# Token columns that are read alternately from two sets of 128 in a decoder trunk's matmuls

## The chip, the core and the metric

The kernel runs on one core of a Trainium2 chip. The time is the device time of one execution in microseconds (us). The kernel before took 2052.29 us in the median of three runs (2049.8 to 2054.64). TensorE (PE in the profile) multiplies, ScalarE (ACT) and VectorE (DVE) work element by element, GpSimd (POOL) does a few sums and issues some DMAs, SyncE (SP) issues the loads. PEld is the loading of the stationary operand on TensorE.

## The reference

One sequence of 256 tokens with 2048 features, in float32, passes through two layers. Cut to what matters:

```python
for i in range(2):
    h = rmsnorm(x, mix_norm[i])
    x = x + (rglru_block(h) if i == 0 else dilated_attention_block(h))
    h = rmsnorm(x, mlp_norm[i])
    x = x + square(relu(h @ w1[i])) @ w2[i]        # 2048 -> 8192 -> 2048
return rmsnorm(x, final_norm)

# rglru_block:  xb, gb = split(h @ w_in)           # 2048 -> 2 x 2560
#               xb = causal_conv4(xb)
#               r, i = sigmoid(blockdiag(xb, w_a)), sigmoid(blockdiag(xb, w_x))   # 10 blocks of 256
#               scan over the tokens of a * h + u, times gelu(gb), @ w_out
# attention:    q, k, v = h @ w_qkv; partial rotary on q, k; three dilated windows mixed; @ w_o
```

All weights are read once; the output is float32.

## The kernel before, in words

Every product is taken in three matmuls. Both operands are split into a high and a low part of a shorter float type (`fp32r`); high x high, high x low and low x high are added up in a PSUM bank. A weight block of 128 rows by 2048 (1 MB, a *unit*) is loaded into `raw`, ScalarE writes its high part `whi` (L132), VectorE subtracts to give the low part `wlo` (L136). Units run in a written order, with loads five units ahead and the split two to three units ahead.

There are two families of products:

- *Weights stand, tokens move* (`stand_w`, L286). The output is features by tokens. For each of 16 blocks of 128 input features, a 128x128 block of the weights is loaded as the stationary operand and the 256 tokens pass by: `whi` with the tokens' high part, `whi` with their low part, `wlo` with their high part. One unit is 48 matmuls of 256 columns. The projections of the recurrent block (40 units), the first MLP products (64 per layer) and q and k (32) go this way. `gate_run` (L437) does the same with the gates' blocks, 24 matmuls for each of ten heads.
- *Tokens stand, weights move* (`stand_x`, L298). The output is tokens by features; 512 columns of weights pass by. The second MLP products, v and the output projections go this way. Here the weights lie in an order made on the host, so that `in_turn` (L318) reads them alternately from two halves that are 256 elements apart, column by column, and the result comes out in natural order. In the last unit of the program (`last_half`, L957) such matmuls have 256 columns each.

The tokens of a stage lie in four tiles `xT`, each with four blocks of 512 columns: the high parts of 256 tokens, then the low parts. They come from `transpose_chunk` (L234): TensorE transposes 128x128 pieces of the residual `xc` into a PSUM bank `tr`, ScalarE empties it with the norm's scale into `xg` (L244), and `hilo` (L216) writes the high part on ScalarE and the low part on VectorE. For the first stage the transposed input comes from the host. For the gates, `conv_split` (L414) splits the convolution's output `c` into `chl` the same way. In the attention, q and k leave PSUM by two copies of 32 rows on ScalarE (L752, L753) and a product with the rotary table on VectorE (L762).

In the steady part of an MLP, one *group* is eight `stand_w` units and fourteen products of the other family with combined weights (sums of blocks, made on VectorE at L653 and by DMA); VectorE adds the results from the banks into `xc` (L657). Each MLP has seven such groups, after eight `stand_w` units at its start. All three engines run their instructions in the order in which the program writes them.

Of the kernel before, what the change touches and what calls it, by code (L numbers as in the profile page):

```python
# [10 lines left out]
F32 = mybir.dt.float32  # L11
F32R = mybir.dt.float32r
AF = mybir.ActivationFunctionType
# [4 lines left out]
S = 256  # L18
# [7 lines left out]
KD = D // 128  # L26
# [50 lines left out]
def trunk(ctx: ExitStack, tc: tile.TileContext, a: dict, out: bass.AP):  # L77
    nc = tc.nc
# [45 lines left out]
    def new_hi(i):  # L124
        split[i] = (cut_tile(i, "hi", HI_BUFS),)
# [65 lines left out]
    def after(n, fn, *args):  # L191
        later.setdefault(now[0] + n, []).append((fn, args))
# [7 lines left out]
    def mm(o, l, r, start, stop):  # L200
        nc.tensor.matmul(o, l, r, start=start, stop=stop, skip_group_check=True)  # L201
# [6 lines left out]
    def pcol(name, j):  # L208
        at = PC[name][0] + j
        return par[:, at:at + 1]  # L210
# [5 lines left out]
    def hilo(hi_out, lo_out, src):  # L216
        nc.scalar.activation(hi_out, src, AF.Copy)
        nc.vector.tensor_sub(lo_out, src, hi_out.bitcast(F32))  # L218

    def new_xT(n):  # L220
        t = perm.tile([P, 4, 512], F32R, name=f"xT{n}")
        state["xT", n] = t
        return t

    def xT(k):
        return state["xT", k // 4][:, k % 4, :]

    def new_xg(n):
        if scope[0] in ("mlp", "end"):
            t = lru.tile([P, UW], F32, name=("q12", "q22")[n % 2])  # L230
            return t[:, 0:4 * S].rearrange("p (k s) -> p k s", k=4)
        return lru.tile([P, 4, S], F32, name="xg", bufs=2)

    def transpose_chunk(n, gname):  # L234
        state["kick"] = True
        xg = new_xg(n)
        for b in range(2):
            tr = psum.tile([P, 2, S], F32, name="tr", bufs=2)
            for k in range(2):
                c = (2 * b + k) * 128  # L240
                for t in range(NT):
                    nc.tensor.transpose(tr[:, k, t * 128:(t + 1) * 128], xc[n][:, t, c:c + 128], ident)  # L242
            for k in range(2):
                nc.scalar.activation(xg[:, 2 * b + k, :], tr[:, k, :], AF.Identity,  # L244
                                     scale=pcol(gname, 4 * n + 2 * b + k))
        t = new_xT(n)
        for h in range(2):
            s = slice(2 * h, 2 * h + 2)
            hilo(t[:, s, 0:256], t[:, s, 256:512], xg[:, s, :])

    def square_sum(n, ts=range(NT)):
        sq = state["ssq"]
# [33 lines left out]
    def stand_w(ps, u, ks, w_at, first, last):  # L286
        hi, lo = split[u]
        cut = 128 if state.pop("kick", False) else 256
        for j, k in enumerate(ks):
            x = xT(k)  # L290
            s = slice((w_at + j) * 128, (w_at + j + 1) * 128)
            for at in range(0, 256, cut):
                mm(ps[:, at:at + cut], hi[:, s], x[:, at:at + cut], first and j + at == 0, False)
            cut = 256
            mm(ps, hi[:, s], x[:, 256:512], False, False)
            mm(ps, lo[:, s], x[:, 0:256], False, last and j == len(ks) - 1)

    def stand_x(acc, u, get, ks, first, last, ts=range(NT)):  # L298
        hi, lo = split[u]
        state["kick"] = False  # L300
        for j, k in enumerate(ks):
            x = get(k)
            s = slice(j * 512, (j + 1) * 512)
            for t in ts:
                xh, xl = x[:, t * 128:(t + 1) * 128], x[:, 256 + t * 128:256 + (t + 1) * 128]
                end = j == len(ks) - 1
                three(acc[t], xh, xl, hi[:, s], lo[:, s], first and j == 0, last and end,
                      state["border"] and end and t == ts[-1])

    def three(bank, xh, xl, hi, lo, opens, closes, border):  # L310

        mm(bank, xh, in_turn(hi), opens, False)
        mm(bank, xh, in_turn(lo), False, False)
        cut = 256 if border else 512
        for at in range(0, 512, cut):
            mm(bank[:, at:at + cut], xl, in_turn(hi, at, cut), False, closes and at + cut == 512)
# [74 lines left out]
    blk = {}  # L391
# [22 lines left out]
    def conv_split(h):  # L414
        if h == 0:
            lru.tile([P, 112], F32, name="space0")
        t = lru.tile([P, 2, 512], F32R, name="chl")
        if h == 0:
            lru.tile([P, 16], F32, name="space1")
        blk[h, "chl"] = t  # L420
        hilo(t[:, :, 0:256], t[:, :, 256:512], blk[h, "c"])

    def gb_done(h, j, ps):
        if j == 0:
# [12 lines left out]
    def gate_run(h, u):  # L437
        hi, lo = split[u]
        x = blk[h, "chl"]
        gp = [psum.tile([P, 2, S], F32, name="g", bufs=2) for _ in range(2)]  # L440
        for g in range(2):
            for n in range(2):
                for k in range(2):
                    at = (g * 2 + k) * 256 + n * 128
                    s = slice(at, at + 128)
                    mm(gp[g][:, n, :], hi[:, s], x[:, k, 0:256], k == 0, False)
                    mm(gp[g][:, n, :], hi[:, s], x[:, k, 256:512], False, False)
                    mm(gp[g][:, n, :], lo[:, s], x[:, k, 0:256], False, k == 1)
        after(0, gate_sig, h, gp)

    def gate_sig(h, gp):
# [276 lines left out]
    scale = HD ** -0.5  # L728
# [19 lines left out]
    def qk_done(h, w, ps):  # L748


        z = lru.tile([P, S], F32, name="z", bufs=2)
        nc.scalar.activation(z[0:32], ps[32:64, :S], AF.Copy)  # L752
        nc.scalar.activation(z[32:64], ps[0:32, :S], AF.Copy)  # L753
        after(1, qk_turn, h, w, ps, z)

    def qk_turn(h, w, ps, z):
        if w == 0:
            att["qk", h] = lru.tile([P, 2, 512], F32R, name="qk", bufs=2)
        y = lru.tile([P, S], F32, name="y", bufs=2)
        rope = att["rope"]  # L760
        nc.vector.tensor_mul(z[0:64], z[0:64], rope[0:64, 1, :])
        nc.vector.tensor_mul(y, ps[:, :S], rope[:, 0, :])  # L762
        nc.vector.tensor_add(y[0:64], y[0:64], z[0:64])
        t = att["qk", h]
        hilo_later(t[:, w, 0:256], t[:, w, 256:512], y)
        if w:
            after(1, att_s, h)

    def hilo_later(hi, lo, src):
        nc.scalar.activation(hi, src, AF.Copy)  # L770
        at_end(nc.vector.tensor_sub, lo, src, hi.bitcast(F32))
# [214 lines left out]
    first = [None] * FIRST  # L986
# [28 lines left out]
    for n in range(NCH):  # L1015
        x = new_xg(n)
        t = new_xT(n)
        if n:
            w = wts.tile([P, UW], F32, name="raw", bufs=RAW_BUFS)
        parts = [slice(m * 512, (m + 1) * 512) for m in range(FIRST)]  # L1020
        raw[n] = [(s, w[:, s]) for s in parts]
        cols = [slice(0, 2), slice(2, 4)] if n == 0 else [slice(0, 4)]
        loads = parts if n == 0 else [slice(0, 1024), slice(1024, 2048)]
        for i in range(max(len(cols), len(loads))):
            if i < len(cols):
                c = cols[i]
                nc.sync.dma_start(x[:, c, :], a["xT"][:, 4 * n + c.start:4 * n + c.stop, :])
            if n or i:
                nc.sync.dma_start(w[:, loads[i]], units[n]["ap"][:, loads[i]])
            else:  # L1030
                nc.sync.dma_start(par, a["par"])
        new_hi(n)
        new_lo(n)
        order = ("x0", "w0", "x1", "x2", "x3", "w1", "w2", "w3") if n == 0 else (
            "x0", "x1", "x2", "w0", "x3", "w1", "w2", "w3")
        for what in order:
            k = int(what[1])
            if what[0] == "w":
                hi_piece(n, k)
                lo_piece(n, k)  # L1040
                continue
            g = pcol("mix0", 4 * n + k)
            nc.scalar.activation(t[:, k, 0:256], x[:, k, :], AF.Identity, scale=g)
            nc.vector.scalar_tensor_tensor(t[:, k, 256:512], x[:, k, :], g, t[:, k, 0:256].bitcast(F32),
                                           op0=OP.mult, op1=OP.subtract)
        for m in range(FIRST):
            stand_w(first[m][3][:, :S], n, range(4 * n, 4 * n + 4), 4 * m, n == 0, n == NCH - 1)
        if n == 1:
            softplus_parts()
# [31 lines left out]
    for at in range(len(items) - 1, -1, -1):  # L1081
        u = items[at][0]
# [44 lines left out]
def _layout(x, mix_norm, mlp_norm, final_norm, mlp_w1, mlp_w2, lru_w_in, lru_conv_w, lru_conv_b,  # L1127
            lru_w_a, lru_b_a, lru_w_x, lru_b_x, lru_lambda, lru_w_out, attn_w_qkv, attn_w_o):
    c = np.ascontiguousarray
# [13 lines left out]
    def turned(w):  # L1143
# [4 lines left out]
    con, rope = _tables()  # L1148
    x2 = x[0]
# [1 line left out]
    begin = w_in[[0, 1, KR, KR + 1]].reshape(4, 128, NCH, 512).transpose(2, 1, 0, 3)  # L1151
    d = {
        "x": c(x2.reshape(NT, 128, D).transpose(1, 0, 2)),
        "xT": c(x2.T.reshape(KD, 128, S).transpose(1, 0, 2)),
        "par": c(np.concatenate([cols(mix_norm[0]), cols(mix_norm[1]), cols(mlp_norm[0]), cols(mlp_norm[1]),
                                 cols(lru_lambda[0]), cols(lru_b_a[0]), cols(lru_b_x[0]), cols(lru_conv_b[0]),
                                 cols(lru_conv_w[0])], 1)),
# [31 lines left out]
```

## Time and profile before

| | |
|---|---|
| median of the runs | 2052.29 us |
| profiled execution, device time | 2051.29 us |
| its span, first to last instruction | 2049.2 us |
| TensorE busy | 2031.2 us, 14231 matmuls |
| weight loads on TensorE busy | 1910.6 us |
| VectorE busy | 1712.1 us, 1927 instructions |
| ScalarE busy | 1278.3 us, 1388 instructions |
| HBM read | 409.58 MB, 201 GB/s over the span |
| granted TensorE clock | 0.999 of full |

A name such as `acc<-xT,whi` tells the tile that is written, then what is read: the moving operand and the stationary one. "128x256" is the size of what passes by. A matmul's own duration runs from its start to the end of its last result and overlaps the next matmul; how fast matmuls follow one another is read from their starts, or from a piece of the chain that counts them.

### The profile page before, as it was taken

The numbers are of one execution on the slowest core, as the hardware profiler recorded it, in microseconds if no ns is written. First come the engines' busy times: TensorE is split into PE (matmuls) and PEld (weight loads), VectorE is DVE, ScalarE is ACT, GpSimd is POOL, SyncE is SP. The second block draws the span as 40 slices with busy tenths as digits, with TensorE's granted clock in tenths as the row PEclk, the third lists the DMA queues.
The fourth block names the chain that finished last, engine by engine and source line by source line (L and its number), as shares of the span: only waits on it lengthen the run. The fifth ranks groups of instructions, "written<-read, shape, count | busy, mean of one in ns | idle before, by whom it ended". The sixth has DMA issues, their size and how long they took to land.

```text
span 2049.2 us, 33880 instructions
## 1 busy us (share of the span) xinstructions
PE 2031.2 (99%) x14231; PEld 1910.6 (93%) x14231; DVE 1712.1 (84%) x1927; ACT 1278.3 (62%) x1388; POOL 87.1 (4%) x83
## 2 busy tenths in 40 slices
PE   9999999999999999999999999999999999999998
PEld 8999988999999999999899999989999999999997
DVE  7988865799999989998557868756999999999985
ACT  7777775566566666656646556555666666666554
POOL 0111100000000000000000000000000000000001
PEclk9999999999999999999999999999999999999999
DMA  8555565678888788777555555556888887887873
GB/s 305 206 199 195 191 213 197 236 240 247 286 260 261 251 269 267 230 253 246 206 190 171 179 185 178 179 197 229 247 247 278 257 266 243 271 274 231 248 251 147
DMA packets 68920, 472.59 MB, mean 231 GB/s; under 512 B 7584, under 2 KB 7712, under 8 KB 13472
## 3 DMA queue, kind: packets, MB, share of 16 engines
q1 hardware_dynamic: 60560, 411.45, 54.9%
q0 software_dynamic: 8064, 58.72, 14.3%
q8 instruction: 111, 1.82, 0.3%
q14 instruction: 41, 0.34, 0.0%
q10 hardware_dynamic: 144, 0.26, 0.0%
HBM read 409.58 MB, written 2.10 MB: 201 GB/s over the span
## 4 chain that ended last, share of the span: by engine, by line
PE 88%; DVE 5%; issue 3%; ACT 2%; DMA 1%; SPq 0%; ACTq 0%; DVEq 0%
PE acc L201 44%; PE g L201 31%; PE tr L201 13%; DVE wlo L136 2%; ACT whi L132 2%; DVE xc L657 1%; DVE qT L653 1%; DMA q<-in_w 0%; DVE aT L572 0%; PE tr L242 0%; DMA xg<-in_xT 0%; PE tr L820 0%; DVE uu L563 0%; ACT xg L244 0%; DVE xT L218 0%
## 5 line engine op out<-in xcount | busy, mean ns | idle before, releaser
L132 ACT ACTIVATE whi<-raw 128x2048 fp32r<-128x2048 f32 (+1 forms) x309 | 569.0, 1844 | 375.7 <-PE acc L201 201.8
L136 DVE TENSOR_TENSOR wlo<-raw,whi 128x2048 fp32r<-128x2048 f32 (+1 forms) x309 | 677.0, 2196 | 96.4 <-ACT whi L132 95.4
L201 PE MATMUL g<-xT,whi 128*128 128x256 f32 x3649 | 627.7, 277 | 0.0
L201 PEld LDWEIGHTS g<-xT,whi 128*128 128x128 f32 x3649 | 550.5, 188 | 0.0
L201 PE MATMUL g<-xT,wlo 128*128 128x256 f32 x1824 | 504.5, 277 | 0.0
L201 PE MATMUL acc<-xT,whi 128*128 128x256 f32 x2724 | 466.6, 277 | 0.2 <-ACT whi L132 0.2
L201 PEld LDWEIGHTS acc<-xT,whi 128*128 128x128 f32 x2724 | 410.9, 188 | 1.3 <-ACT whi L132 1.1
L201 PE MATMUL acc<-xT,wlo 128*128 128x256 f32 x1360 | 376.3, 277 | 0.4 <-DVE wlo L136 0.4
L201 PEld LDWEIGHTS g<-xT,wlo 128*128 128x128 f32 x1824 | 342.5, 188 | 0.4 <-DVE wlo L136 0.4
L201 PE MATMUL acc<-whi,aT 128*128 128x512 f32 (+1 forms) x1064 | 322.6, 378 | 0.0
L132 ACT ACTIVATE whi<-q 128x2048 fp32r<-128x2048 f32 x112 | 214.7, 1917 | 117.8 <-PE g L201 91.9
L136 DVE TENSOR_TENSOR wlo<-q,whi 128x2048 fp32r<-128x2048 f32 x112 | 256.1, 2287 | 26.9 <-ACT whi L132 26.4
L201 PEld LDWEIGHTS acc<-xT,wlo 128*128 128x128 f32 x1360 | 255.3, 188 | 0.9 <-DVE wlo L136 0.8
L201 PEld LDWEIGHTS acc<-whi,aT 128*128 128x128 f32 x1064 | 200.6, 189 | 27.4
L201 PE MATMUL tr<-whi,sT 128*128 128x512 f32 (+1 forms) x728 | 213.7, 366 | 5.5 <-DVE xc L657 4.6
L201 PE MATMUL acc<-wlo,aT 128*128 128x512 f32 (+1 forms) x532 | 200.8, 377 | 0.0
L132 ACT ACTIVATE whi<-qT 128x2048 fp32r<-128x2048 f32 x56 | 107.5, 1920 | 126.5 <-PE g L201 91.5
L201 PEld LDWEIGHTS tr<-whi,sT 128*128 128x128 f32 x728 | 137.4, 189 | 33.9 <-issue 16.0
L201 PE MATMUL tr<-whi,aT 128*128 128x512 f32 (+1 forms) x462 | 140.1, 373 | 0.0
L136 DVE TENSOR_TENSOR wlo<-qT,whi 128x2048 fp32r<-128x2048 f32 x56 | 128.1, 2287 | 7.2 <-ACT whi L132 5.6
L201 PE MATMUL tr<-wlo,sT 128*128 128x512 f32 x336 | 127.4, 379 | 0.0
L201 PEld LDWEIGHTS acc<-wlo,aT 128*128 128x128 f32 x532 | 100.6, 189 | 13.4
(169 smaller groups left out, 2119.6 us busy)
## 6 DMA issues: line engine op xcount, KB each, us to landing
raw<-in_w SPq DMA_DIRECT2D x172, 1024.0 KB, 7.0
q<-in_w SPq DMA_DIRECT2D x84, 1024.0 KB, 8.1
raw<-in_w_in SPq DMA_DIRECT2D x35, 1024.0 KB, 4.9
raw<-in_w_qk SPq DMA_DIRECT2D x32, 1024.0 KB, 4.8
q<-q POOLq DMA_DIRECT2D x28, 1024.0 KB, 12.5
q<-qT POOLq DMA_DIRECT2D x28, 1024.0 KB, 7.0
raw<-in_w_out SPq DMA_DIRECT2D x20, 1024.0 KB, 4.8
raw<-in_w_v SPq DMA_DIRECT2D x16, 1024.0 KB, 4.8
```

Source lines behind the costliest of these rows:

```text
L132: nc.scalar.activation(split[i][0][:, s], r, AF.Copy)
L136: nc.vector.tensor_sub(split[i][1][:, s], r, split[i][0][:, s].bitcast(F32))
L201: nc.tensor.matmul(o, l, r, start=start, stop=stop, skip_group_check=True)
L653: nc.vector.tensor_add(q[to], q[a], q[b])
L657: (nc.vector.tensor_add if sign > 0 else nc.vector.tensor_sub)(x, x, bank[b])
```

## The change

The moving tokens of the first family are read alternately. In a block of 512 columns there now lie, in this order: the high parts of a first set of 128 tokens, their low parts, the high parts of a second set of 128, their low parts. `moving` reads column by column from the first and the second set, 256 elements apart: first set's column 0, second set's column 0, first set's column 1, and so on. The matmuls are otherwise the same, in the same order, with the same sizes.

For a result in the natural order, the first set must hold the even tokens and the second the odd ones. So the host sends the first `xT` sorted; `transpose_chunk` reads every second column of the bank as it empties it (`by_turn`) in both MLPs' stages; `conv_split` reads every second column of `c`. In the attention's stage the two sets stay the first and the last 128 tokens, since v takes them as stationary blocks; q and k then come out of PSUM alternating, and the two copies and the product with the table (L752, L753, L762) put them back in order by reading every second column. Instructions keep their number and their places on all engines.

```diff
@@ transpose_chunk
             for k in range(2):
-                nc.scalar.activation(xg[:, 2 * b + k, :], tr[:, k, :], AF.Identity,
+                order = halves if gname == "mix1" else by_turn
+                nc.scalar.activation(halves(xg[:, 2 * b + k, :]), order(tr[:, k, :]), AF.Identity,
                                      scale=pcol(gname, 4 * n + 2 * b + k))
...
-            hilo(t[:, s, 0:256], t[:, s, 256:512], xg[:, s, :])
+            hilo(part(t[:, s], 0), part(t[:, s], 1), xg[:, s, :].rearrange("p k (t q) -> p k t q", t=2))
+
+    def by_turn(x):
+        return x.rearrange("p (q t) -> p t q", t=2)
+
+    def halves(x):
+        return x.rearrange("p (t q) -> p t q", t=2)
+
+    def part(x, u):
+        return x.rearrange("p k (t u q) -> p u k t q", t=2, u=2)[:, u]
+
+    def moving(x, u):
+        return x.rearrange("p (t u q) -> p u q t", t=2, u=2)[:, u]
@@ stand_w
+            xh, xl = moving(x, 0), moving(x, 1)
             for at in range(0, 256, cut):
-                mm(ps[:, at:at + cut], hi[:, s], x[:, at:at + cut], first and j + at == 0, False)
+                mm(ps[:, at:at + cut], hi[:, s], xh[:, at // 2:(at + cut) // 2], first and j + at == 0, False)
             cut = 256
-            mm(ps, hi[:, s], x[:, 256:512], False, False)
-            mm(ps, lo[:, s], x[:, 0:256], False, last and j == len(ks) - 1)
+            mm(ps, hi[:, s], xl, False, False)
+            mm(ps, lo[:, s], xh, False, last and j == len(ks) - 1)
@@ stand_x
-                xh, xl = x[:, t * 128:(t + 1) * 128], x[:, 256 + t * 128:256 + (t + 1) * 128]
+                if get is xT:
+                    xh, xl = (x[:, (2 * t + i) * 128:(2 * t + i + 1) * 128] for i in range(2))
+                else:
+                    xh, xl = x[:, t * 128:(t + 1) * 128], x[:, 256 + t * 128:256 + (t + 1) * 128]
@@ conv_split
-        hilo(t[:, :, 0:256], t[:, :, 256:512], blk[h, "c"])
+        hilo(part(t, 0), part(t, 1), blk[h, "c"].rearrange("p k (q t) -> p k t q", t=2))
@@ gate_run
-                    mm(gp[g][:, n, :], hi[:, s], x[:, k, 0:256], k == 0, False)
-                    mm(gp[g][:, n, :], hi[:, s], x[:, k, 256:512], False, False)
-                    mm(gp[g][:, n, :], lo[:, s], x[:, k, 0:256], False, k == 1)
+                    xh, xl = moving(x[:, k], 0), moving(x[:, k], 1)
+                    mm(gp[g][:, n, :], hi[:, s], xh, k == 0, False)
+                    mm(gp[g][:, n, :], hi[:, s], xl, False, False)
+                    mm(gp[g][:, n, :], lo[:, s], xh, False, k == 1)
@@ qk_done
-        nc.scalar.activation(z[0:32], ps[32:64, :S], AF.Copy)
-        nc.scalar.activation(z[32:64], ps[0:32, :S], AF.Copy)
+        nc.scalar.activation(halves(z[0:32]), by_turn(ps[32:64, :S]), AF.Copy)
+        nc.scalar.activation(halves(z[32:64]), by_turn(ps[0:32, :S]), AF.Copy)
@@ qk_turn
-        nc.vector.tensor_mul(y, ps[:, :S], rope[:, 0, :])
+        nc.vector.tensor_mul(halves(y), by_turn(ps[:, :S]), halves(rope[:, 0, :]))
```

The first stage's split (L1043, L1044) writes the new order too, and the host sorts the transposed input.

More of the change, by code (lines that the diff above doesn't have):

```diff
@@ L1042, in trunk @@
             g = pcol("mix0", 4 * n + k)
-            nc.scalar.activation(t[:, k, 0:256], x[:, k, :], AF.Identity, scale=g)
-            nc.vector.scalar_tensor_tensor(t[:, k, 256:512], x[:, k, :], g, t[:, k, 0:256].bitcast(F32),
+            high, low = (part(t, u)[:, k] for u in range(2))
+            nc.scalar.activation(high, halves(x[:, k, :]), AF.Identity, scale=g)
+            nc.vector.scalar_tensor_tensor(low, halves(x[:, k, :]), g, high.bitcast(F32),
                                            op0=OP.mult, op1=OP.subtract)
@@ L1153, in _layout @@
         "x": c(x2.reshape(NT, 128, D).transpose(1, 0, 2)),
-        "xT": c(x2.T.reshape(KD, 128, S).transpose(1, 0, 2)),
+        "xT": c(x2.T.reshape(KD, 128, 128, 2).transpose(1, 0, 3, 2)).reshape(128, KD, S),
         "par": c(np.concatenate([cols(mix_norm[0]), cols(mix_norm[1]), cols(mlp_norm[0]), cols(mlp_norm[1]),
```

## The prediction

> **What bounds the kernel now.** I read the shares of busy time first, then the table of stretches, then the chain that ended last.
>
> ```profile
> PE 2031.2 (99%) x14231; PEld 1910.6 (93%) x14231; DVE 1712.1 (84%) x1927; ACT 1278.3 (62%) x1388; POOL 87.1 (4%) x83
> PE 88%; DVE 5%; issue 3%; ACT 2%; DMA 1%; SPq 0%; ACTq 0%; DVEq 0%
> 448.00:529.00 81.00, 80.61 (x560) 75.43 (x558) 75.65 (x73) 50.41 (x42) 3.42 (x4) 1.00 0.82 260
> ```
>
> TensorE is busy 99% of the span and carries 88% of the chain. The third row is one of the 14 like groups of the two MLPs (stretch, its length, then PE, PEld, DVE and ACT busy): PE idles 0.4 us of 81, VectorE 5.35 us. The granted clock is 1.00. So time is the number of matmuls times the interval at which they start, and only that interval can move it. VectorE is next in line.
>
> The changed products are these groups (the by-form list, whose last columns are busy us, mean ns of one, idle before):
>
> ```profile
> L201 PE MATMUL g<-xT,whi 128*128 128x256 f32 x3647 | 627.4, 277 | 0.0
> L201 PE MATMUL g<-xT,wlo 128*128 128x256 f32 x1824 | 504.5, 277 | 0.0
> L201 PE MATMUL acc<-xT,whi 128*128 128x256 f32 x2716 | 465.6, 277 | 0.2 <-ACT whi L132 0.2
> L201 PE MATMUL acc<-xT,wlo 128*128 128x256 f32 x1360 | 376.3, 277 | 0.4 <-DVE wlo L136 0.4
> L201 PE MATMUL g<-chl,ghi 128*128 128x256 f32 x160 | 28.7, 281 | 0.0
> L201 PE MATMUL g<-chl,glo 128*128 128x256 f32 x80 | 22.5, 281 | 0.0
> ```
>
> The program has 200 such units (40 projections, 128 first MLP products, 32 for q and k) of 16 tiles times 3, so 9600 matmuls; the rows show 9547 of them (another tile name holds 48), plus 240 of the gates. The 277 ns cannot be used: it is one matmul from start to end, and they overlap. What counts is start to start. The chain gives it for long runs, for a unit alone between other products, and for a triple:
>
> ```profile
> 128.26 21.78 PE acc L201 x192
> 486.58 5.48 PE g L201 x48
> 1493.50 16.34 PE g L201 x144
> ```
>
> That is 113.4, 114.2 and 113.5 ns for 256 columns.
>
> **What an alternating read costs.** The kernel already has one. The other family of products (weights moving) reads its 512 columns from two places 256 elements apart, column by column, which is the very distance that the change gives the tokens. Its pace, and that of its 256-column form in the last part of the program, where each matmul again has stationary data of its own:
>
> ```profile
> 1017.18 0.59 PE L201 MATMUL acc<-whi,xT 128*128 128x512 f32 x2
> 1017.61 0.38 PE L201 MATMUL acc<-wlo,xT 128*128 128x512 f32 x1
> 1017.83 0.59 PE L201 MATMUL acc<-whi,xT 128*128 128x512 f32 x2
> 2037.13 0.28 PE L201 MATMUL acc<-wlo,aT 128*128 128x256 f32 x1
> ...
> 2039.14 0.28 PE L201 MATMUL acc<-wlo,aT 128*128 128x256 f32 x1
> 612.52 0.38 PE L201 MATMUL tr<-whi,sT 128*128 128x256 f32 x2
> 612.74 0.40 PE L201 MATMUL g<-xT,whi 128*128 128x256 f32 x2
> ```
>
> From 1017.18 to 1017.83 three matmuls of 512 start: 216 ns each, or 108 per 256 columns. From 2037.13 to 2039.14 there are six triplets, 18 matmuls: 111.7 ns. At 612.52 two of 256 columns take 0.22 us, 110 each; they follow a matmul of 512 and both use the same tokens as stationary. A plain read at 113.4 is slower than all three. The plain read also depends on which tile it reads; the gates, on a tile of 512 columns for each of two halves, start like this:
>
> ```profile
> 100.90 0.28 PE L201 MATMUL g<-chl,glo 128*128 128x256 f32 x1
> ...
> 103.37 0.28 PE L201 MATMUL g<-chl,glo 128*128 128x256 f32 x1
> ```
>
> Seven triplets in 2.47 us: 117.6 ns.
>
> I take 111.7 for the changed matmuls, since it has everything they will have: 256 columns, two places 1024 bytes apart, and a new 128x128 stationary block each time, one after the other for 2 us. The ends are 110 (the pair at 612.52) and 117.6 (the worst 256-column pace shown with units this dense); 108 has half as many weight loads and is not a candidate.
>
> **The sum.** No instruction is added or removed, on any engine, and none changes its place in its queue; access patterns change.
>
> - MLP groups. Each has a triple and five units alone: 16.34 + 5 x 5.48 = 43.7 us for 384 matmuls. At 111.7 they take 42.9. Saving 0.8 us, 14 groups: 11.2 us.
> - The other 88 units: four run at the start, behind the loads, and I give them nothing. The other 84 run long, 4032 matmuls at 113.4 - 111.7 = 1.7 ns: 6.9 us.
> - Gates: 240 x (117.6 - 111.7) = 1.4 us.
>
> Together 19.5 us. Against it stand the places where PE waits for something that does not get faster:
>
> ```profile
> 1418.55 9.31 DMA q<-in_w
> 1449.84 0.48 PE L201 MATMUL acc<-wlo,sT 128*128 128x512 f32 x1 [0.64 <-DVE wlo L136]
> 526.00:545.00 19.00, 18.94 (x112) 16.94 (x110) 18.96 (x15) 12.83 (x10) 0.86 (x1) 1.00 0.71 207
> PE tr L201 <- DVE xc L657: 4.6, 14, 0.3
> ```
>
> From 1418.55 the chain runs over a load and then VectorE until PE waits at 1449.84; some 200 changed matmuls lie in between (17 us of one stream and a unit of 48), whose 0.3 us is lost there. In an MLP group VectorE works without a pause for 19 us (18.96 busy in the third row), and at the end of it PE waits up to 0.3 us for a bank that VectorE empties at L657 (last row: us in total, times, longest). One unit of 48 lies in that stretch, so up to 48 x 1.7 = 0.1 us of a group's saving turns into a longer wait, 1.1 us over 14 groups. I take 0.7. **Forecast of the saving: 18.5 us.** The VectorE itself is no wall: 75.65 us of work against a group that becomes 80.2.
>
> **What the sorting costs.** Four kinds of instructions on ScalarE and VectorE now read every second element, or write in blocks of 128:
>
> ```profile
> L244 ACT ACTIVATE xg<-tr,par 128x256 f32<-128x256 f32 x28 | 10.9, 469 | 0.0
> L762 DVE TENSOR_TENSOR y<-acc,rope 128x256 f32<-128x256 f32 x32 | 13.1, 409 | 0.0
> L752 ACT ACTIVATE z<-acc 32x256 f32<-32x256 f32 x32 | 12.0, 376 | 0.8
> L218 DVE TENSOR_TENSOR chl<-c,chl 128x512 fp32r<-128x512 f32 x10 | 6.8, 684 | 0.9 <-ACT chl L217 0.9
> 1390.03 1.57 ACT L244 ACTIVATE q<-tr,par 128x256 f32<-128x256 f32 x4 [2.67 <-PE tr L242]
> 1392.16 1.29 DVE L218 TENSOR_TENSOR xT<-q,xT 128x512 fp32r<-128x512 f32 x2 [2.46 <-ACT xT L217]
> 1394.43 0.39 PE L201 MATMUL acc<-xT,whi 128*128 128x256 f32 x2
> ```
>
> The trace holds no read of every second element by these engines. Their price lies between nothing and, as an estimate from these rows, once more the duration. Doubled, L762 and the sub of L218 cost VectorE 13.1 + 6.8 us over 600 us in which PE is the bound, and L752, L753 and L244 cost ScalarE (62% busy) some 40 us. This hides behind TensorE's stream. The one tight place is an MLP's start: the last quarter of the tokens is ready at 1392.16 + 1.29 = 1393.45 and first read at 1394.43, so 1.0 us of cover. If the emptying (1.57) doubled, PE would wait 0.6 us, at two MLP starts 1.2 us. I take the lower end, nothing, since the count of elements is the same and no row shows these engines depend on more, and keep 1.2 in the range.
>
> The sum goes against the profiled execution's 2051.29 us (span 2049.2, 2.1 around it): 2032.8. The runs' median lies 1.0 above that execution, so the forecast for it is **2034 us**, 0.9% less. Its own range: at 111.0 ns the saving would be 25 us, at 112.7 about 10, so 2027 to 2042.
>
> **The rivals.**
>
> *No weight-load share left (6%).* The pair at 612.52 is the true pace of an alternating read and the last part of the program is held at 111.7 by something that is not there in the long streams. Then 9408 matmuls (196 units) save 113.6 - 110 = 3.6 ns, 34 us, the gates 1.8: 2016. For it speaks that two matmuls in a row did it; against it that every longer row of 256 columns shows 111 to 112. [...]
>
> *The read is not what holds the plain stream (12%).* The 113.4 comes from the tiles' places or from loading whi and wlo as stationary, and remains. For it: the gates read plainly too, at 117.6, so the pattern alone does not set the pace; and no row has whi as stationary with an alternating read. Then only the gates may gain: 2051 to 2053, no change.
>
> *The alternation meets the weight load (9%).* Here, unlike in the 512-column products, every matmul has a weight load over its whole length, and the tokens' two places may lie badly to the weights' place. Place: every changed matmul; price: the gates' pace, 117.6 - 113.6 = 4.0 ns x 9600 = 38 us, so 2090; it decides from 114.0 ns on (0.4 x 9600 = 4 us, 0.2%). Against it: the last part has the same density of loads and runs at 111.7. [...]
>
> **How the numbers follow.** Forecast 73%, the rivals 6, 12 and 9%. A measurement of this kernel tells 0.2% (4 us) from no change. Faster: 73 + 6 = 0.79; same 0.12; slower 0.09. The range 2022 to 2052 holds the forecast with its tails and most of the case of no change, about 8 in 10; below it lies the 2016, above it the loss.
>
> **What would show it.** In the changed profile the long runs of 192 in the chain should take 21.44 us instead of 21.78, a triple 16.08 instead of 16.34, the eight units of a group 42.9 together; the gates' triplets 0.335 us instead of 0.353; the 512-column rows still 216 ns. An MLP group should shrink from 81 by 0.7 to 0.8 us with VectorE's 75.65 unchanged. L244, L762 and L218 show the price of sorting directly; a new wait of PE at the MLPs' starts would show that it is not hidden. I am wrong if the runs of 192 still take 21.7, or if the groups shrink less than their units do, which would put the loss on VectorE's waits.

## The result and the profile after

The changed kernel took **2031.05 us** (median of four runs, 2030.33 to 2034.56), the kernel before 2052.24 beside it on the same chip (four runs, 2049.8 to 2054.64): a ratio of 0.990, 95% interval 0.9883 to 0.9917. The profiled span went from 2049.2 to 2028.7 us, 20.5 less. Forecast were 2034 us and a saving of 18.5.

First the shares of busy time and one group of the first MLP in the table of stretches (stretch, its length, then PE, PEld, DVE and ACT busy), of the changed kernel:

```profile
PE 2009.9 (99%) x14231; PEld 1891.7 (93%) x14231; DVE 1714.6 (85%) x1927; ACT 1280.0 (63%) x1388; POOL 88.0 (4%) x83
444.20:524.26 80.06, 79.66 (x560) 74.77 (x558) 75.41 (x73) 50.48 (x42) 3.42 (x4) 1.00 0.81 261
```

The matmuls are as many as before and TensorE is still full (99% busy). A group holds the same 560 matmuls and the same work of VectorE, in less time. Then the pieces of the chain that count matmuls, of the changed kernel:

```profile
128.10 21.44 PE acc L201 x192
463.74 16.08 PE g L201 x144
...
944.45 16.08 PE g L201 x144
...
1083.40 10.72 PE acc L201 x96
...
1478.17 16.08 PE g L201 x144
...
1958.87 16.08 PE g L201 x144
```

192 matmuls in 21.44 us, 144 in 16.08, 96 in 10.72: 111.7 ns each time. Plain, these pieces gave 113.4 and 113.5. The same places in the kernel before:

```profile
467.65 16.33 PE g L201 x144
...
953.28 16.33 PE g L201 x144
...
1979.08 16.33 PE g L201 x144
```

With 128.26 and 1493.50 from the prediction, these rows say where the time was won. Up to the run at 128 it is 0.2 us; to the first MLP's first triple 3.9 (467.65 less 463.74); to its seventh 8.8; to the second MLP's first triple 15.3; to its seventh 20.2; and 20.5 at the end. Six groups of the first MLP take 485.63 us before and 480.71 after, six of the second 485.58 and 480.70: 0.82 and 0.81 us won for each group.

The gates and the sorting, in the by-form list of the changed kernel (busy us, mean ns, idle before):

```profile
L201 PE MATMUL g<-chl,ghi 128*128 128x256 f32 x160 | 27.3, 276 | 0.0
L245 ACT ACTIVATE xg<-tr,par 128x256 f32<-128x256 f32 x28 | 10.8, 469 | 0.0
L782 DVE TENSOR_TENSOR y<-acc,rope 128x256 f32<-128x256 f32 x32 | 13.0, 407 | 0.0
L772 ACT ACTIVATE z<-acc 32x256 f32<-32x256 f32 x32 | 12.0, 376 | 0.8
L217 ACT ACTIVATE chl<-c 128x512 fp32r<-128x512 f32 x10 | 8.0, 804 | 5.9 <-DVE c L428 4.4 <-PE g L201 1.3
L218 DVE TENSOR_TENSOR chl<-c,chl 128x512 fp32r<-128x512 f32 x10 | 7.4, 736 | 1.7 <-ACT chl L217 1.7
```

And the row of the kernel before that answers to the fifth:

```profile
L217 ACT ACTIVATE chl<-c 128x512 fp32r<-128x512 f32 x10 | 6.3, 629 | 8.7 <-DVE c L409 4.6 <-PE g L201 4.1
```

The three kinds that read every second column out of PSUM cost what they did (469, 407 and 376 ns against 469, 409 and 376). The two that read every second column of `c`, which lies in SBUF, became dearer: 629 to 804 ns on ScalarE, 684 to 736 on VectorE. That is 1.8 and 0.5 us in all, spread over 250 us. It is the read that costs: with the same blocks written but `c` read plainly (experiment 1) the two take 630 and 685 ns. Of PE's waits in the changed kernel, those for VectorE's sums and for `wlo` (us in total, times, longest):

```profile
PE tr L201 <- DVE xc L677: 4.6, 14, 0.3
PE acc L201 <- DVE wlo L136: 0.8, 3, 0.3
PE g L201 <- DVE wlo L136: 0.6, 1, 0.6
```

The wait for a bank in each group is what it was. The 0.64 us at the second MLP's start has gone; the waits on `wlo` all lie in the first 104 us. That stretch in the table of stretches, the kernel before and then the changed one:

```profile
0.00:104.00 104.00, 102.15 (x858) 98.40 (x859) 89.34 (x152) 78.71 (x115) 7.58 (x8) 1.00 0.71 253
```

```profile
0.00:104.00 104.00, 100.89 (x855) 96.59 (x856) 88.63 (x152) 78.54 (x114) 7.41 (x8) 1.00 0.70 252
```

PE idles 3.1 us there after the change and 1.9 before. In this pair of executions the faster matmuls bring nothing in the first 104 us; how much of that repeats, the traces of the experiments tell further down.

### The profile page after: what moved, and what is told of

It reads as the page before. It is cut to its first block, busy times and chain, and to the rows that moved or that the text cites. A ratio compares the mean times of both kernels' runs of the same rounds, so it can differ in the third digit from the quotient of the medians.

```text
span 2028.7 us, 33879 instructions
## 1 busy us (share of the span) xinstructions
PE 2009.9 (99%) x14231; PEld 1891.7 (93%) x14231; DVE 1714.6 (85%) x1927; ACT 1280.0 (63%) x1388; POOL 88.0 (4%) x83
## 4 chain that ended last, share of the span: by engine, by line
PE 73%; DVE 17%; issue 6%; ACT 2%; DMA 1%; SPq 0%; DVEq 0%; ACTq 0%
PE acc L201 42%; PE g L201 24%; DVE wlo L136 8%; PE tr L201 7%; DVE qT L673 3%; DVE xc L677 2%; ACT whi L132 2%; DVE aT L592 1%; DVE uu L583 1%; DMA raw<-in_w_in 1%; PE tr L242 0%; DVE c L428 0%; DMA xg<-in_xT 0%; PE tr L840 0%; ACT xg L245 0%
## 5 line engine op out<-in xcount | busy, mean ns | idle before, releaser
L201 PE MATMUL g<-xT,whi 128*128 128x256 f32 x3649 | 615.9, 276 | 0.0
L201 PE MATMUL acc<-xT,whi 128*128 128x256 f32 x2724 | 458.7, 276 | 0.4 <-ACT whi L132 0.4
L201 PEld LDWEIGHTS g<-xT,wlo 128*128 128x128 f32 x1824 | 350.9, 192 | 1.3 <-DVE wlo L136 1.3
L201 PEld LDWEIGHTS acc<-xT,wlo 128*128 128x128 f32 x1360 | 261.6, 192 | 2.0 <-DVE wlo L136 1.8
```

## The experiments

The theory was that **the order in which the moving columns are read sets the pace**: two neighbours in a row are slow (113.4 ns in the kernel before), a change of place at every column is fast (111.7 ns in the changed one). The rivals: the new *layout* of `xT` is the cause; the *distance* of 1024 bytes is; the *weight load* between matmuls is, and the read only seems to be. A position below counts elements of 4 bytes, so 16 bytes are four positions. Ratios are against the kernel before, run beside each set.

**1. The layout without the alternation.** Sets and blocks lie as in the change, but the columns are read 128 and then 128, and nothing is sorted.

```diff
-        return x.rearrange("p (t u q) -> p u q t", t=2, u=2)[:, u]     # moving
+        return x.rearrange("p (t u q) -> p u t q", t=2, u=2)[:, u]
-        return x.rearrange("p (q t) -> p t q", t=2)                    # by_turn
+        return x.rearrange("p (t q) -> p t q", t=2)
```

> The changed layout (high and low parts of 128 tokens in turn) is kept, but the columns are read plainly, 128 of the first set and then 128 of the second, and no token is sorted. If the alternation makes the pace: runs of 192 in the chain back at 21.78 us (113.4 ns), gates about 117 ns, the kernel at 2050 to 2053 us. If the new layout of the tiles makes it: 21.44 us, 2031 us.

2051.56 us against 2051.46 before, ratio 1.0001 (0.9991 to 1.001). The chain of this kernel, and its waits:

```profile
129.32 21.78 PE acc L201 x192
```

```profile
PE acc L201 <- DVE wlo L136: 1.5, 3, 1.0
```

The layout alone does nothing: 113.4 ns again. The alternation is the whole gain. The wait of 1.0 us on `wlo` is the one at the second MLP's start; it does not go with the pace, as is shown further down.

**2. A shorter distance.** The blocks lie as before the change (256 high, 256 low), and the two sets are 128 elements apart.

```diff
-        return x.rearrange("p (t u q) -> p u q t", t=2, u=2)[:, u]     # moving
+        return x.rearrange("p (u t q) -> p u q t", t=2, u=2)[:, u]
```

> The old layout (256 high parts, then 256 low parts), read alternately from places 128 elements (512 bytes) apart instead of 256 (1024 bytes). If any alternation will do: 111.7 ns, runs of 192 in 21.44 us, the kernel at 2031 us. If the distance of 1024 bytes matters: between 112.5 and 117 ns, 2040 us or more.

2031.88 us, ratio 0.9904 (0.9887 to 0.992).

```profile
127.52 21.44 PE acc L201 x192
```

The same 111.7 ns at half the distance.

**3. The other family read plainly.** The changed kernel, with the 512 columns of weights in natural order.

```diff
-        return w.rearrange("p (t q) -> p q t", t=2)[:, at // 2:(at + n) // 2, :]
+        return w[:, at:at + n]
```

> The changed kernel, but the other family (weights moving, 512 columns) reads its columns plainly; weights lie in natural order. If a plain read loses per column, as the 4.4 ns between 113.4 and 109 for 256 columns say: 216 becomes about 225 ns, 3900 matmuls, 2065 us. [...] If a plain read costs nothing in itself: 2031 us.

2068.99 us, ratio 1.0082 (1.0067 to 1.0097), so some 38 us above the changed kernel. The timeline of this kernel (start, us, engine, line, operation):

```profile
1025.52 0.62 PE L201 MATMUL acc<-whi,xT 128*128 128x512 f32 x2
...
1026.20 0.62 PE L201 MATMUL acc<-whi,xT 128*128 128x512 f32 x2
```

Three matmuls of 512 in 0.68 us: 227 ns, where the alternating read takes 216. Plain reading costs 11 ns for each 512 columns; per 256 that is 5.5, more than the 1.8 which the tokens' matmuls lose in their long runs (113.45 less 111.7). So these runs are held at 111.7 by something else, and the next pair looked for that.

**4. Half the weight load.** In 15 of the 16 blocks of a unit only 64 columns stand instead of 128. Half of each unit's sums are left unfinished; the moving columns and the number of matmuls are unchanged. Once with the alternating read, once with the plain one of the kernel before.

```diff
+            n = 128 if j == 0 and first else 64
-            s = slice((w_at + j) * 128, (w_at + j + 1) * 128)
+            s = slice((w_at + j) * 128, (w_at + j) * 128 + n)
-            mm(ps, hi[:, s], xl, False, False)
+            mm(ps[0:n], hi[:, s], xl, False, False)
```

> The changed kernel; in each unit only the first of 16 blocks of weights stands with its 128 columns, the other 15 with 64 of them (half the features' sums stay unfinished; this is what it leaves out). The moving reads stay as they are. If the 111.7 ns are set by the weight load: 109 ns, as the pair behind a 512-column matmul, runs of 192 at 20.95 us, 23 us less, 2008 us. If the moving read sets them: 111.7 ns, 2031 us.

> The kernel before (plain reads) with the same halved weight loads, the same sums left out. If a plain read loses by meeting the weight load, half the load halves the loss: from 113.4 to 111 to 112 ns, 2030 us. If the plain read is slow by itself: 113.3 ns as before, 2050 us.

Alternating 2011.53 us, ratio 0.9798 (0.977 to 0.9827); plain 2069.18, ratio 1.0079 (1.005 to 1.0108). The chain of the alternating one, then of the plain one:

```profile
127.23 20.99 PE acc L201 x192
```

```profile
105.09 22.05 PE acc L201 x192
```

109.3 ns and 114.8. With the alternating read, 64 standing columns in place of 128 give back 2.4 ns (111.7 to 109.3), and the author puts these down to the weight load; how long a load of 64 columns takes was not read. Half the standing columns also means half the rows of results that are written. Against these as the cause speak the matmuls of 512 columns, which write all 128 rows at 216 ns, or 108 for 256 columns; a load comes once for each matmul, whatever its columns (14231 of each in the profile). The plain read gains nothing from fewer standing columns (114.8 ns against 113.4), and so is not held by the load. That it even became slower by 1.4 ns was not expected, and no run explains it.

**5. Which order is fast.** Five kernels, with one more edit of the same kind: the tokens of a 256-column block are put so that this order of positions gives the natural result. The gates' `c` is split in halves there, 20 pairs of instructions instead of 10.

```diff
-        return x.rearrange("p (t u q) -> p u q t", t=2, u=2)[:, u]     # moving
+        return x[:, u * 256:(u + 1) * 256].rearrange("p (b t q) -> p b q t", t=2, q=8)   # 0,8,1,9,...
+        ... .rearrange("p (b t q) -> p b q t", t=2, q=4)   # 0,4,1,5,...
+        ... .rearrange("p (b t q) -> p b q t", t=2, q=2)   # 0,2,1,3,...
+        ... .rearrange("p (t b q) -> p b t q", t=2, q=4)   # 0 to 3, 128 to 131, 4 to 7, ...
+        ... .rearrange("p (t b q) -> p b t q", t=2, q=2)   # 0,1,128,129,2,3,...
```

> Old layout, read alternately from two sets that are 8 elements (32 bytes) apart, in blocks of 16. If any change of place between two columns will do: 111.7 ns, 2031 us. If the two places must lie far apart: 113 to 117 ns, 2050 us or more.

> [...]

> [...]

> Old layout, two sets 128 elements (512 bytes) apart, but four columns (16 bytes) of one and then four of the other. If each column must come from the other place than the one before: 113 ns or more, 2050 us. If it is enough that the places change often: 111.7 ns, 2031 us.

> Old layout, two sets 512 bytes apart, two columns of one and two of the other. By fours cost 126 ns and column by column 111.7. If a run of columns from one place is what costs, and a longer one more: 113 to 120 ns, 2050 to 2110 us. If a switch of place between runs is what costs: twice as many switches as by fours, above 126 ns, 2180 us or more. If two in a row are still free: 111.7 ns, 2031 us.

The run of 192 in the chains of the five, in this order (eight positions apart; four apart; two apart; by fours; by twos):

```profile
127.14 21.44 PE acc L201 x192
```

```profile
128.08 21.44 PE acc L201 x192
```

```profile
129.10 21.78 PE acc L201 x192
```

```profile
114.05 24.33 PE acc L201 x192
```

```profile
111.78 31.58 PE acc L201 x192
```

| order of positions | bytes to the next column (steps forward) | ns per matmul | us | ratio (95%) |
|---|---|---|---|---|
| 0,256,1,257 (the change) | 1024 | 111.7 | 2031.05 | 0.990 (0.9883 to 0.9917) |
| 0,128,1,129 | 512 | 111.7 | 2031.88 | 0.9904 (0.9887 to 0.992) |
| 0,8,1,9 | 32 | 111.7 | 2030.34 | 0.989 (0.9861 to 0.9919) |
| 0,4,1,5 | 16 | 111.7 | 2031.91 | 0.9892 (0.9874 to 0.991) |
| 0,2,1,3 | 8, 4 | 113.4 | 2052.68 | 0.9995 (0.9985 to 1.0005) |
| 0,1,2,3 (the plain read, experiment 1) | 4 | 113.4 | 2051.56 | 1.0001 (0.9991 to 1.001) |
| 0 to 3, 128 to 131, 4 to 7 | 4, 4, 4, 512 | 126.7 | 2175.76 | 1.0598 (1.0567 to 1.0629) |
| 0,1,128,129,2,3 | 4, 512 | 164.5 | 2567.64 | 1.25 (1.2478 to 1.2523) |

The border lies between 8 bytes (113.4 ns) and 16 bytes (111.7). 0,4,1,5 takes every column from another group of four than the one before; 0,2,1,3 stays in the group of four and behaves like the plain read (113.4 ns both). So alternation as such is worth nothing; every order that left the group of 16 bytes at every column was fast (111.7 ns). Whether the group itself counts, or the length of a step, which in 0,4,1,5 is 16 bytes forward or 12 back at all but one column in eight, these orders do not separate. Staying in a group for two or four columns and then going far away is much worse than the plain read (164.5 and 126.7 ns against 113.4). Per matmul, 63 changes of set cost 13.3 ns by fours (126.7 less 113.4) and 127 changes cost 51 by twos. This is no fixed price for a change: 0.21 ns each in the one, 0.40 in the other. Why the read behaves like this, no run shows.

**6. Fewer matmuls in place of faster ones.** The high and low tokens go past one load of `whi` as 512 columns, into both halves of a bank. First for all units, with the second half left out of the sum; then for the later 34 of the recurrent block's units and all 32 of q and k, with the halves added: ScalarE copies one and VectorE adds the other.

```diff
-                mm(ps[:, at:at + cut], hi[:, s], xh[:, at // 2:(at + cut) // 2], first and j + at == 0, False)
+                mm(ps, hi[:, s], x.rearrange("p (t u q) -> p u q t", t=2, u=2), first and j == 0, False)
-            mm(ps, hi[:, s], xl, False, False)
-            mm(ps, lo[:, s], xh, False, last and j == len(ks) - 1)
+            mm(ps[:, 0:256], lo[:, s], xh, False, last and j == len(ks) - 1)
@@ only in the second kernel
+        nc.scalar.activation(w, ps[:, S:2 * S], AF.Copy)
+        nc.vector.tensor_add(w, w, ps[:, :S])
```

> The changed kernel, with the high weights loaded once per triple: one matmul of 512 columns takes the tokens' high and low parts into the two halves of a bank, then the low weights take 256 columns. The second half (high weights times the tokens' low parts) is never added to the result, which is what this kernel leaves out. A triple should take 216 + 110 to 112 = 327 ns instead of 335, so 200 units x 16 x 8 ns = 25 us less, 2006 us, if VectorE and ScalarE keep up; 2031 us or a little under if they do not (VectorE's 75.6 us against a group of 79).

> The changed kernel with the high weights loaded once per triple (512 columns into two halves of a bank) in 34 units of the recurrent block and the 32 of q and k, where VectorE has room; ScalarE copies the second half and VectorE adds the first, so the result is whole. 66 units x 16 x 7.5 ns = 7.9 us less than the changed kernel, 2023 us, if the 66 additions (0.4 us each) hide; VectorE is 91 to 98% busy between 25 and 100 us, so up to 2 us of it may be lost there: 2023 to 2026 us. If the additions do not hide: 2031 us or more.

Without the addition 2011.41 us, ratio 0.9801 (0.9786 to 0.9815):

```profile
127.62 20.96 PE acc L201 x128
```

64 pairs in 20.96 us are 327.5 ns where three matmuls took 335. The pace is as expected, but the kernel gained 20 us on the changed one and not 25; where the rest was lost was not followed. With the addition it is 2124.98 us, ratio 1.0346 (1.0331 to 1.036), 94 above the changed kernel where a gain was expected. PE's waits in that kernel, then the waits of all engines between 100 and 290 us:

```profile
PE tr L862 <- DVE s L857: 30.9, 14, 3.2
PE acc L201 <- DVE wlo L136: 30.7, 15, 3.6
PE g L201 <- DVE glo L136: 8.0, 8, 1.2
```

```profile
DVE xb L425 <- ACT xb L424: 38.2, 13, 5.6
ACT gb L424 <- DVE i L524: 29.9, 6, 5.0
ACT th L516 <- DVE th L515: 28.4, 7, 4.1
```

These are 69.6 us; the changed kernel has 0.8 of them (`acc` waiting for `wlo`), so 69 of the 94 are new waits. ScalarE and VectorE wait for each other: ScalarE's copy into `gb` (L424) waits until VectorE has read that tile for the head before (L524), VectorE's addition (L425) waits for ScalarE's copy, and in VectorE's queue the split of the next weights stands behind the addition. Neither engine is full, as two stretches of this kernel show (columns as above, the eighth the granted clock):

```profile
100.00:290.00 190.00, 162.55 (x977) 146.73 (x976) 145.24 (x208) 125.16 (x168) 23.81 (x12) 0.96 0.45 155
1140.00:1390.00 250.00, 221.24 (x1224) 195.75 (x1223) 176.91 (x337) 142.83 (x244) 0.00 (x0) 0.96 0.43 150
```

VectorE is busy 145 of 190 us and ScalarE 125, and PE idles 27. The other 25 us are not idle time: over the whole program PE is busy 2036.1 us against the changed kernel's 2009.9, though it runs 1056 matmuls fewer. In these stretches the granted clock was 0.96 instead of 1.00; 4% of their 440 us would be 18 us, an estimate. What makes up the rest of the slower matmuls was not taken apart. Another place in the queues for the two instructions was not tried. Of the kernels that compute the whole result, the changed one and its variants at 16, 32 and 512 bytes are the fastest, with no difference between them that can be told.

## Why the prediction was right

**The pace.** 111.7 ns was taken from the last part of the program, because it had 256 columns, an alternating read and a new stationary block each time. It measured 111.7 in runs of 192, triples and runs of 96 alike. The choice against 110 (rival of 6%) was right, and experiment 4 points to why: with 64 standing columns in place of 128 the pace is 109.3, so the author takes it that the load of a stationary block for each matmul holds it at 111.7.

**The MLP groups**, 14 x 0.8 = 11.2 us: the groups shrank by 0.82 and 0.81, so 14 of them give 11.4. (Without rounding the rows give 0.85 for a group; not every unit alone takes the 5.48 us that stands in the sum, the chain of the kernel before has 5.45 and 5.46 too.) Taken off for VectorE were 0.7 us. That term was wrong: the bank wait is 4.6 us in 14 times, as before. VectorE is busy without a pause at the end of a group (19.00 of the 19.00 us from 521.60 in the changed kernel), but PE's wait there did not grow.

**The other 84 units**, 6.9 us, and **the gates**, 1.4. The gates run at 111.7, their triplet at 0.335 us:

```profile
101.14 0.39 PE L201 MATMUL g<-chl,ghi 128*128 128x256 f32 x2
101.47 0.39 PE L201 MATMUL g<-chl,ghi 128*128 128x256 f32 x2
```

The sums do not come out in the places where they were booked. Up to the run at 128 us there are 20 units and four heads of gates. The forecast gave nothing to the first four units, and 1.3 us to the other 16 with 0.6 to the gates; measured are 0.2 in this pair of executions. Much of that is scatter. The run starts at 128.26, 129.32 and 129.10 in three kernels of the plain pace (before, experiment 1, the order 0,2,1,3) and at 128.10, 127.52, 127.14 and 128.08 in four of the alternating pace (the change, then 512, 32 and 16 bytes): about 1 us apart within each kind, and 1.2 apart in the mean. So of the 1.9 some 0.7 did not come, as an estimate from these seven starts, and the other 1.0 is the luck of one pair. One piece of the 0.7 is seen in the changed kernel:

```profile
79.82 0.38 PE L201 MATMUL acc<-xT,wlo 128*128 128x256 f32 x1 [0.34 <-DVE wlo L136]
```

All four alternating kernels wait here for VectorE's split, 0.30 to 0.34 us, and none of the three plain ones. So "behind the loads" ends later than after four units: that step of the prediction failed, at a price of less than 1 us. Whether the dearer reads of `c` (0.23 us for each head) have a part in this was not separated.

**A plain pace that was not seen** makes up for part of it. At the attention's start, between products of the other family, the first four units of the kernel before ran like its gates, not like its long runs:

```profile
1059.00 0.40 PE L201 MATMUL acc<-xT,whi 128*128 128x256 f32 x2
...
1064.65 0.40 PE L201 MATMUL acc<-xT,whi 128*128 128x256 f32 x2
```

16 triplets in 5.65 us: 117.7 ns. It stays so for all 192 matmuls, and after the change they take 111.7: 1.2 us, of which the sum held 0.3 (192 times 1.7 ns, as for any of the 84 units). The plain read has at least two paces on the same tile (113.4 and 117.7 ns), and the alternating read has shown one (111.7).

**The start of the second MLP** was booked at a loss of 0.3 us, on the view that the wait for `wlo` behind a load stays where it is. In the changed kernel it is not there. The timeline at that place:

```profile
1435.12 0.38 PE L201 MATMUL acc<-whi,sT 128*128 128x512 f32 x1
1435.34 0.38 PE L201 MATMUL acc<-wlo,sT 128*128 128x512 f32 x1
```

These follow at 0.22 us, where the kernel before had 1.01 (1448.83 to 1449.84): a gain of 0.8. It cannot be put down to the faster matmuls. The second of these two matmuls in a kernel of the plain pace (0,2,1,3), then in one of the alternating pace (16 bytes):

```profile
1449.58 0.38 PE L201 MATMUL acc<-wlo,sT 128*128 128x512 f32 x1
```

```profile
1436.31 0.48 PE L201 MATMUL acc<-wlo,sT 128*128 128x512 f32 x1 [0.80 <-DVE wlo L136]
```

Of the seven traces above, two of the three plain ones and one of the four alternating ones have the wait (0.64, 1.04 and 0.80 us). So it comes and stays away at either pace; what decides it was not found, and whether the pace makes it rarer, seven traces cannot tell. For the forecast this gain was luck.

So the saving came out 2.0 us above the 18.5 (20.5 in the span): 0.2 more from the groups and 0.7 not lost to VectorE, 1.1 for the second MLP's start (0.8 in place of -0.3) and 0.8 for the attention's first units, less 1.7 in the first 128 us. These make 1.1; the other 0.9 was not followed to its place. The luck at the second MLP's start and the bad luck of about 1.0 in the first 128 us nearly cancel.

**What the sorting costs.** "Nothing" was right for all reads from PSUM and wrong for the reads of `c` from SBUF (28% more on ScalarE, 8% on VectorE, inside the bounds of nothing and double). The cover at the MLPs' starts was not needed.

**The rivals.** "The read is not what holds the plain stream" falls with the first experiment together with the change: same tiles, same loads, only the order of columns, 113.4 and 111.7. "The alternation meets the weight load" falls too: the load is met, at 111.7, but costs 2.4 ns (111.7 less the 109.3 of experiment 4), if these are the load's, and not the 4.0 above the plain pace that were feared.

## What to carry to other kernels

Where TensorE is the bound, read the pace from start to start for each operand pattern, at several places: a pace of 113 to 118 ns where the same shape elsewhere runs at 111.7 is an opening. For a moving operand of 4-byte elements, an order in which every column lies in another 16 bytes than the column before was the fastest here (111.7 ns; 113.4 plainly), and one that stays for two or four columns and then goes far was the slowest (164.5 and 126.7 ns); the sorting can go into an instruction that empties PSUM, where it cost nothing (469 ns before and after). An addition on two engines that are not full can still cost far more than it brings, if each must wait for the other (94 us against some 8, which is 66 units of 16 triplets by 335 less 327.5 ns).

## What the runs showed that had not been expected

- By twos with 512 bytes between took 164.5 ns for 256 columns, 47% more than the change, and by fours 126.7; plain reading takes 113.4.
- With a plain read, half the stationary columns made the pace slower (114.8 against 113.4 ns); with the alternating read, faster (109.3 against 111.7).
- The plain read ran at 113.4 in one stage and at 117.7 in another, on tiles of the same form, and kept each for at least 192 matmuls.
- Reading every second 4-byte element cost ScalarE 28% more out of SBUF (629 to 804 ns for 512 elements) and nothing out of PSUM (469 and 469 for 256).
